# Six gate projections moved among the key and query projections of a hybrid layer, with later query transposes, another order of the first loads and of the last stores

## The chip, the cores and the metric

The kernel runs on one core of a Trainium2 chip. The metric is the time of one execution on the device in microseconds (us). The engines of the core are named as in the profile: PE (TensorE, matrix products; its weight loads are PEld), DVE (VectorE), ACT (ScalarE), POOL (GpSimd) and SP (SyncE, which issues the DMAs here). Each engine works its own instructions off in a fixed order.

## What is computed

One layer of an encoder over 1024 tokens of width 1024, and a final norm. All data are float32.

```python
h = rms_norm(x, mix_norm_w)
proj = h @ w_in
dn_qkv, dn_z, dn_b, dn_a, a_q, a_k, a_v, x_q, gate_logits = jnp.split(proj, IN_OFFSETS, axis=-1)
# A: DeltaNet: conv + SiLU, unit q/k, chunks of 64 with a triangular solve, a scan over
#    16 chunks forward and one backward, norm, SiLU gate                        -> y_dn
# B: attention, 8 query heads, 2 key heads, per-head norm and rotary            -> y_att
# C: cross-attention of 4 heads into 256 memory tokens                          -> y_x
...
ys = jnp.stack([y_dn, y_att, y_x], axis=2)
yb = jnp.einsum("bsnc,ncd->bsnd", ys, w_branch)
gates = jax.nn.sigmoid(gate_logits.reshape(b_, s_, N_BRANCH, D_MODEL))
merged = jnp.sum(gates * yb, axis=2)
x = x + merged @ w_out
x = x + jnp.square(jax.nn.relu(rms_norm(x, ffn_norm_w) @ w_up)) @ w_down
return rms_norm(x, final_norm_w)
```

The triangular solve is per chunk: `triangular_solve(lmat, rhs)` with `lmat` 64 x 64, unit diagonal; there are 128 of them (16 chunks, 4 heads, 2 directions).

## The kernel before

**Products.** Every float32 operand is split into a high and a low part (`split`, L140 to L142: ACT casts the high part, DVE or POOL subtracts it), and a product is three matmuls: high by high, high by low, low by high. `wunit` (L146) loads one unit of weights, 128 columns of all 1024 rows, 512 KB, and splits it; the low part goes to DVE, or to POOL while `wlo[0]` is set. A projection of one unit on one half of the tokens (512) is 24 matmuls of 128x512 into one PSUM tile of the pool `ps_mm`, which has two buffers.

**Order of the program.** The phases are written one after the other, and a scheduler then orders the instructions of each engine by dependencies and modelled times; it may move work of a later phase ahead. Only in attention (from L994 on) is PE's order kept as written.

1. L254 to L285: x is loaded in 8 tiles of 128 tokens, normalised (ACT sums the squares, L223; DVE scales with the norm weight, L278), transposed by PE and split into `hTh[f]`, `hTl[f]` (f: the half of the tokens).
2. L301 to L430: decays, convolution and DeltaNet's matrices per chunk (`conv_tile` L393, `prep` L464), whose results go to device memory (`xs_d`, `kn_d`, `qT_d`, `at_d`).
3. Driver, L663 to L671: one step of `keys()` or `queries()` (24 steps: 8 blocks of keys, 16 of queries), then one step of `other` (the z gate, memory rows and the cross queries, tile `xh`/`xl`). A step projects 128 tokens (`ps_dn`), takes norm and rotary (`rope_norm` L552, on ACT, POOL, DVE), writes the parts `qhl`/`khl`, and the four transposes of them on PE (L84, tile `ps_t`), an eviction on ACT and the stores by SP stand at the head of the next step. `wlo[0]` is POOL here.
4. L693 to L710: the triangular solve, for all 128 chunks at once, one per partition, on DVE: for each of 62 columns a product (L705, tile `tm`) and an addition (L706, tile `X`), then a product with `bcol` (L708). X is loaded from `xs_d` before, stored to `ts_d` after, and read back by chunk as `tf` and `Tr`.
5. L739 to L830: the scan over the chunks (`ps_sp` and `ps_sm` on PE).
6. L870 to L1016: attention, in 64 steps, with cross-attention.
7. L1023 to L1160: the three branch products times gates (y tiles read back as `y_raw`, split into `g_yh`, `g_yl`; gates as `g_l`, through a pool of two buffers), output projection, MLP, final norm, stores.

**Gate projections.** 48 tiles of 24 matmuls (3 branches, 8 units, 2 halves) are written as the generator `gates()`, and `fill(n)` emits its next n matmuls. A finished tile is evicted (tanh, to `g_d`) when the next portion is drawn. 7 tiles are emitted at once after the driver and the scan's code (`GATES[0]`), 3 behind the scan, 33 in portions of 3, 4, 5 and 12 in attention, and the 5 left over in `for _ in gt` (L1019), between attention and the branches.

**Queues.** SP issues all DMAs in one order. A store that isn't ready holds up the loads behind it. At the end the stores of the last two blocks of 128 rows stand in halves in this queue.

Of the kernel before, what the change touches and what calls it, by code (L numbers as in the profile page):

```python
# [9 lines left out]
F32 = mybir.dt.float32  # L10
# [12 lines left out]
GATES = (7, 3)  # L23
# [63 lines left out]
def hybrid_block(tc, x, mem, mix_norm_w, w_in, dn_conv_w, dn_a_log, dn_dt_bias, dn_norm_w, q_norm_w, k_norm_w,  # L87
# [33 lines left out]
    ld(out=ca, in_=ca_d)  # L121
# [5 lines left out]
    act.copy(out=identr, in_=ident)  # L127
# [108 lines left out]
    ld(out=wdn, in_=dn_norm_w.rearrange("o d -> d o"))  # L236
    dve.tensor_scalar(out=wdn, in0=wdn, scalar1=0.5, scalar2=None, op0=ALU.mult)
# [17 lines left out]
    first = {}  # L255
    wbc = p0.tile([P, D], F32, name="wbc", bufs=1)
    for m in range(8):
        if m == 0:
            xts = []
            for i in range(8):  # L260
                xt = p0.tile([P, D], F32, name="xt", tag="xt", bufs=8)
                ld_rows(xt, x, i)
                xts.append(xt)
                if i == 0:
                    ld(out=wbc, in_=mix_norm_w.broadcast_to([P, D]))
                if i == 1:
                    braw = wst.tile([P, 8, 64], F32, name="w_raw", tag="w_raw")
                    bhl = tkp.tile([P, 8, 128], F32R, name="b_hl", tag="t_hi", bufs=1)
                    ld(out=braw, in_=w_in[:, C_BA:C_BA + 64].rearrange("(k p) c -> p k c", p=P))
                    split(bhl[:, :, 0:64], bhl[:, :, 64:128], braw)  # L270
                if i == 3:
                    wlo[0] = gp
                    for ct in (4, 0):
                        first[ct] = wunit(w_in[:, ct * P:(ct + 1) * P], 8, P)
                    wlo[0] = None
# [9 lines left out]
    st.close()  # L285

# [7 lines left out]
    R = [slice(0, 64), slice(64, 128)]  # L294

# [97 lines left out]
    def conv_tile(ct):  # L393
# [4 lines left out]
        for f in range(2):  # L398
            ps = ps_mm()
            proj_ch(ps, wh, wl, f)  # L400
# [175 lines left out]

    def keys():
        wh, wl = wtok(C_AKV)
        for m in range(8):
# [5 lines left out]
            khl = tkp.tile([P, 512], F32R, name="khl", tag="qhl")[:, :384].rearrange("p (g a d) -> p g a d", g=2, a=3)  # L585
            rope_norm(khl[:, :, 1], khl[:, :, 0::2], ps[:, 0:128].rearrange("p (g d) -> p g d", g=2), 2, rope, m, 1.0 / 64, EPS)
            yield
            pst = ps_t(F32R)
# [8 lines left out]
    def queries():  # L597
        for g in range(2):
            wh, wl = wtok(C_AQ + g * 256)
            for m in range(8):  # L600
# [6 lines left out]
                for h in range(4):  # L607
                    pe.transpose(pst[:, h * P:(h + 1) * P], qhl[:, h].rearrange("p a d -> p (a d)"), identr)
# [57 lines left out]
    for _ in other:  # L666
        pass
# [571 lines left out]
```

## Time and profile before

| | us |
|---|---|
| median of 3 runs | 1977.83 (1975.19 to 1977.91) |
| profiled execution | 1976.33 |
| its span | 1974.5 |
| PE busy | 1900.6 (96%) |
| DVE busy | 1169.2 (59%) |
| ACT busy | 731.8 (37%) |
| POOL busy | 397.2 (20%) |

The span is the time from the first to the last record of the profile; the profiled execution's own time is 1.8 us longer. Busy time is the sum over an engine's instructions, and shares are averages over stages that differ much: the table of stretches further below shows that DVE is busy for nearly all of one of them. In a row of the timeline stand the start, the duration, engine, line, operation, output and input, and in brackets the idle time before it with what ended it.

### The profile page before, as it was taken

How to read it: one execution, taken by the hardware profiler on the slowest of the kernel's cores; microseconds unless marked ns; L12 is line 12 of the kernel's file. 1: busy time of each engine (PE TensorE's matmuls, PEld its weight loads, DVE VectorE, ACT ScalarE, POOL GpSimd, SP SyncE). 2: the span in 40 equal slices, each digit the busy share in tenths (PEclk: the TensorE clock that was granted, in tenths of full speed). 3: DMA queues.
4: the chain of work that ended last, by engine and by line, in shares of the span. 5: the costliest groups of instructions: out<-in, count | busy, mean ns of one | idle time of the engine just before them, and what ended most of it. 6: DMA issues, size and time to landing. Idle time of an engine off the chain costs nothing.

```text
span 1974.5 us, 26282 instructions
## 1 busy us (share of the span) xinstructions
PE 1900.6 (96%) x10229; PEld 1611.6 (82%) x10229; DVE 1169.2 (59%) x1701; ACT 731.8 (37%) x1453; POOL 397.2 (20%) x309
## 2 busy tenths in 40 slices
PE   6999897799999999999999999999999999999997
PEld 5888787688998888888888878888888888888885
DVE  4778879993576666666635463444443444444445
ACT  4344343332555666666642131321121212112124
POOL 3003657851251000000000520100010101001013
PEclk9999998899999999999999999999999999999998
DMA  8235743447654222222146455231111102121113
GB/s 170 76 107 149 226 139 110 118 127 243 191 163 133 85 94 75 86 75 86 59 150 201 157 180 161 74 120 40 55 54 33 54 33 65 43 64 46 41 43 86
DMA packets 232893, 207.82 MB, mean 105 GB/s; under 512 B 44800, under 2 KB 196544, under 8 KB 232256
## 3 DMA queue, kind: packets, MB, share of 16 engines
q1 hardware_dynamic: 232768, 206.13, 34.7%
q8 instruction: 81, 1.33, 0.3%
q14 instruction: 44, 0.36, 0.1%
HBM read 148.91 MB, written 57.18 MB: 104 GB/s over the span
## 4 chain that ended last, share of the span: by engine, by line
PE 74%; DVE 6%; POOL 3%; DMA 2%; issue 2%; ACT 1%; SPq 0%; POOLq 0%; DVEq 0%; ACTq 0%
PE ps L81 40%; PE ps_mm L81 20%; PE ps_t L84 3%; PE ps_sm L81 3%; PE ps_t L81 3%; PE ps_s L81 3%; PE ps_sp L81 2%; DVE tm L705 2%; DVE X L706 1%; POOL r_t L560 1%; DMA w_raw<-in_w_out_dram 1%; POOL r_t L561 1%; POOL r_rs L138 0%; DMA X<-xs_d 0%; DVE o L1152 0%
## 5 line engine op out<-in xcount | busy, mean ns | idle before, releaser
L81 PE MATMUL ps_mm<-hTh,w_hi 128*128 128x512 f32 x704 | 286.1, 406 | 3.5 <-ACT hTh L141 3.4
L81 PE MATMUL ps_mm<-hTl,w_hi 128*128 128x512 f32 x704 | 283.9, 404 | 0.0
L81 PE MATMUL ps_mm<-hTh,w_lo 128*128 128x512 f32 x704 | 277.7, 395 | 2.4 <-POOL w_lo L142 2.4
L1140 DVE TENSOR_TENSOR o<-o,ps 128x512 f32<-128x512 f32 (+1 forms) x257 | 171.3, 683 | 97.0 <-PE ps L81 95.5
L81 PE MATMUL ps<-hfh,w_hi 128*128 128x512 f32 x512 | 199.6, 391 | 0.0
L81 PE MATMUL ps<-wdh,al 128*128 128x512 f32 (+1 forms) x514 | 199.6, 389 | 0.0
L81 PE MATMUL ps<-wdl,ah 128*128 128x512 f32 (+1 forms) x514 | 199.6, 389 | 0.0
L81 PE MATMUL ps<-hfl,w_hi 128*128 128x512 f32 x512 | 199.6, 390 | 0.0
L81 PE MATMUL ps<-hfh,w_lo 128*128 128x512 f32 x512 | 199.5, 390 | 0.0
L142 POOL TENSOR_TENSOR wdl<-w_raw,wdh 128x1024 fp32r<-128x1024 f32 x32 | 76.4, 2397 | 601.1 <-ACT wdh L141 601.1
L81 PE MATMUL ps<-wdh,ah 128*128 128x512 f32 (+1 forms) x514 | 188.7, 389 | 0.0
L1132 ACT ACTIVATE f_r<-ps 128x512 f32<-128x512 f32 x64 | 38.1, 595 | 363.7 <-PE ps L81 363.7
L142 DVE TENSOR_TENSOR w_lo<-w_raw,w_hi 128x1024 fp32r<-128x1024 f32 x78 | 100.0, 1282 | 121.0 <-ACT w_hi L141 120.6
L141 ACT CAST w_hi<-w_raw 128x1024 fp32r<-128x1024 f32 x96 | 100.9, 1051 | 171.6 <-PE ps_mm L81 104.0
L1133 DVE TENSOR_TENSOR f_r<-f_r 128x512 f32<-128x512 f32 x64 | 55.3, 865 | 183.3 <-ACT f_r L1132 183.3
L81 PEld LDWEIGHTS ps_mm<-hTh,w_lo 128*128 128x128 f32 x704 | 133.7, 190 | 28.0 <-POOL w_lo L142 2.6
L81 PEld LDWEIGHTS ps_mm<-hTh,w_hi 128*128 128x128 f32 x704 | 133.7, 190 | 27.9 <-ACT hTh L141 3.8
L81 PEld LDWEIGHTS ps_mm<-hTl,w_hi 128*128 128x128 f32 x704 | 133.9, 190 | 20.2
L1072 POOL TENSOR_TENSOR g_acc<-g_acc,g_l 128x512 f32<-128x512 f32 x28 | 41.4, 1481 | 509.8 <-ACT g_yh L141 475.4
L142 DVE TENSOR_TENSOR ptl<-ps_t,pth 128x512 fp32r<-128x512 f32 x128 | 86.6, 687 | 60.0 <-ACT pth L141 59.7
L81 PEld LDWEIGHTS ps<-wdh,al 128*128 128x128 f32 x514 | 96.6, 188 | 19.9
L81 PEld LDWEIGHTS ps<-wdh,ah 128*128 128x128 f32 x514 | 96.5, 188 | 19.8
(288 smaller groups left out, 4045.9 us busy)
## 6 DMA issues: line engine op xcount, KB each, us to landing
w_raw<-in_w_in_dram SPq DMA_DIRECT2D x50, 512.0 KB, 4.1
w_raw<-in_w_up_dram SPq DMA_DIRECT2D x32, 512.0 KB, 4.1
w_raw<-in_w_down_dram SPq DMA_DIRECT2D x32, 512.0 KB, 3.6
g_d<-gt SPq DMA_DIRECT2D x48, 256.0 KB, 2.0
g_l<-g_d SPq DMA_DIRECT2D x24, 512.0 KB, 3.4
w_raw<-in_w_branch_dram SPq DMA_DIRECT2D x12, 512.0 KB, 4.1
y_raw<-y_d SPq DMA_DIRECT2D x12, 512.0 KB, 3.6
xt<-in_x_dram SPq DMA_DIRECT2D x16, 256.0 KB, 9.9
```

The lines of the kernel that those rows point to most:

```text
L81: return self._put(self.tc.nc.tensor.matmul(*a, **k))
L84: return self._put(self.tc.nc.tensor.transpose(*a, **k))
L141: act.copy(out=hi, in_=src)
L142: (eng or dve).tensor_tensor(out=lo, in0=src, in1=hi.bitcast(F32), op=ALU.subtract)
L560: gp.tensor_tensor(out=t1, in0=x0, in1=bc(tab[:, 0, m], 1, nh), op=ALU.mult)
L561: gp.tensor_tensor(out=t2, in0=x0, in1=bc(tab[:, 1, m], 1, nh), op=ALU.mult)
L705: dve.tensor_tensor(out=t, in0=bc(X[:, j + 1:, j], 2, j), in1=bc(X[:, j, 0:j], 1, n), op=ALU.mult)
L706: dve.tensor_tensor(out=X[:, j + 1:, 0:j], in0=X[:, j + 1:, 0:j], in1=t, op=ALU.add)
L1072: (dve if bi == 2 and mt > 5 else gp).tensor_tensor(out=acc[mt][:, c], in0=acc[mt][:, c], in1=t, op=ALU.add)
L1132: act.activation(out=r, in_=ps, func=AF.Relu)
L1133: dve.tensor_tensor(out=r, in0=r, in1=r, op=ALU.mult)
L1140: dve.tensor_tensor(out=o[m][:, c], in0=o[m][:, c], in1=ps, op=ALU.add)
```

## The change

`GATES` is (6, 3). `gates()` and `fill()` are defined ahead of the driver loop, and after every fourth of its 24 steps one gate tile (24 matmuls) is emitted; their weights are split on POOL. With these 6 tiles none is left for L1019. The transposes of a step go into a list `turns` and are emitted two steps later, with four `qhl` and three `qst` buffers. At the start x's first tile is loaded first; the norm weight comes as one row and is spread by two matmuls with a row of ones and two copies; the units for channels 4 and 0 are loaded between x's tiles; the b and a columns and `wdn` come after x; and the first half of the projections for 4 and 0 is emitted ahead of the decays. At the end blocks 6 and 7 get their factors first, then 7 and 6 are scaled, and the first half of each is stored through ACT's queue.

```diff
-GATES = (7, 3)
+GATES = (6, 3)
...
+    xts = [p0.tile([P, D], F32, name="xt", tag="xt", bufs=8) for _ in range(8)]
...
+    ld_rows(xts[0], x, 0)
+    ld(out=wrow, in_=mix_norm_w)
+    ld(out=ca, in_=ca_d)
+    for i in range(1, 4):
+        ld_rows(xts[i], x, i)
+    for c in range(0, D, 512):
+        ps = ps_mm()
+        pe.matmul(ps, lhsT=one1, rhs=wrow[:, c:c + 512], start=True, stop=True)
+        act.copy(out=wbc[:, c:c + 512], in_=ps)
+    act.copy(out=identr, in_=ident)
+    wlo[0] = gp
+    first[4] = wunit(w_in[:, 4 * P:5 * P], 8, P)
+    for i in range(4, 6):
+        ld_rows(xts[i], x, i)
+    first[0] = wunit(w_in[:, 0:P], 8, P)
+    for i in range(6, 8):
+        ld_rows(xts[i], x, i)
...
-                if i == 0:
-                    ld(out=wbc, in_=mix_norm_w.broadcast_to([P, D]))
...
+    head = {}
+    for ct in (4, 0):
+        head[ct] = ps_mm()
+        proj_ch(head[ct], *first[ct], 0)
...
+    turns = []
+
+    def turn(hl, nh, put):
+        def go():
+            pst = ps_t(F32R)
+            for i, part in enumerate(nh(hl)):
+                pe.transpose(pst[:, i * P:(i + 1) * P], part.rearrange("p a d -> p (a d)"), identr)
+            st = xp.tile([P, 512], F32R, name="qst", tag="qst", bufs=3)
+            act.copy(out=st, in_=pst.bitcast(F32))
+            put(st)
+        turns.append(go)
...
-    for _ in chain(keys(), queries()):
-        next(other, None)
...
+    for i, _ in enumerate(chain(keys(), queries())):
+        next(other, None)
+        if i % 4 == 3:
+            fill(24)
+        if i > 1:
+            turns.pop(0)()
...
+    def store(q, m, c):
+        for h, j in enumerate((m, 15 - m)):
+            q.dma_start(out=out[j * 64:(j + 1) * 64, c], in_=o[m][h * 64:(h + 1) * 64, c])
+
...
+        if m > 5:
+            store(act, m, slice(0, 512))
...
+        if m > 5:
+            store(nc.sync, m, slice(512, 1024))
+        else:
             ld_rows(o[m], out, m, store=True)
...
+    for m in (6, 7):
+        rs3[m] = factor(m, len(cs) - 7 + m)
+    finish(7)
     finish(6)
-    finish(7)
```

SP's queue at the place where the solve's input is loaded: `xs_d` is its source in device memory, `kab` and `qst` are keys on their way out, `vt` values. Before:

```order
L97 DMA at_d7_117<-dd_1968 128x512
L97 DMA vz_d_124<-vt_2235 128x128
L97 DMA vz_d_124<-vt_2326 128x128
L97 DMA xs_d_118<-dd_1968 64x8x64 x2
L97 DMA ka_d_122<-kab_2121 256x1x128
L97 DMA kb_d_123<-kab_2121 256x1x128
L97 DMA vz_d_124<-vt_2411 128x128
L97 DMA X_4243<-xs_d_118 128x4096
```

And in the changed kernel:

```order
L97 DMA at_d7_115<-dd_1977 128x512
L97 DMA vz_d_122<-vt_2226 128x128
L97 DMA vz_d_122<-vt_2317 128x128
L97 DMA xs_d_116<-dd_1977 64x8x64 x2
L97 DMA X_4436<-xs_d_116 128x4096
L97 DMA bcol_4438<-bt_d_118 8x1x64 x2
L97 DMA ka_d_120<-qst_2288 256x1x128
L97 DMA kb_d_121<-qst_2288 256x1x128
```

The key stores stand behind the load of X now.

PE's queue around the first scan matmul (`ps_sp` from `tf`; the next takes `Tr`, which ACT copies from its result). Before, where `ps_mm_5893`, `5927` and `5955` are gate projections of 24 matmuls each:

```order
L81 MATMUL ps_mm_5927<-hTl0_151,w_hi_5921 128x512
L81 MATMUL ps_sp_4433<-ca_73,tf_4422 64x64 x4
L81 MATMUL ps_mm_5927<-hTh0_149,w_lo_5922 128x512
...
L81 MATMUL ps_mm_5955<-hTl1_152,w_hi_5921 128x512
L81 MATMUL ps_sp_4442<-vn_4426,Tr0_4406 128x128 x4
L81 MATMUL ps_sp_4459<-ca_73,tf_4448 64x64 x4
L81 MATMUL ps_mm_5955<-hTh1_150,w_lo_5922 128x512
```

And in the changed kernel, where `ps_t_4423` are the transposes of the last block of queries, and `ps_mm_4195` and `4280` projections of 24 matmuls:

```order
L84 MATMUL ps_t_4423<-identr_74,qhl_4259 128x128 x4
L81 MATMUL ps_mm_4195<-hTh0_147,w_hi_4190 128x512
...
L81 MATMUL ps_mm_4280<-hTh1_148,w_lo_4191 128x512
L81 MATMUL ps_sp_4626<-ca_73,tf_4615 64x64 x4
L81 MATMUL ps_sp_4635<-vn_4619,Tr0_4599 128x128 x4
L81 MATMUL ps_sp_4652<-ca_73,tf_4641 64x64 x2
L81 MATMUL ps_mm_4314<-hTh1_148,w_hi_3928 128x512
```

The matmuls on `Tr` follow those on `tf` at once. Counted over PE's queue from the end of DeltaNet's preparation to the first matmul of the scan, 397 matmuls of 128x512 stand there before and 356 in the changed kernel. DVE's queue from the first column step of the solve to its last product has 225 instructions before and 215 in the changed kernel; inside the scan PE's queue goes 12 times from scan matmuls to gate matmuls or back before, and 75 times in the changed kernel.

PE's queue behind the last attention matmul (`vz`: values). Before, the five remaining gate projections end with `ps_mm_10262`, and the first branch product follows:

```order
L81 MATMUL ps_mm_10262<-hTl1_152,w_hi_10228 128x512
L81 MATMUL ps_mm_10262<-hTh1_150,w_lo_10229 128x512
L81 MATMUL ps_mm_10331<-g_yh_10300,w_hi_10326 128x512
L81 MATMUL ps_mm_10331<-g_yl_10301,w_hi_10326 128x512
L81 MATMUL ps_mm_10331<-g_yh_10300,w_lo_10327 128x512
L81 MATMUL ps_mm_10331<-g_yh_10306,w_hi_10326 128x512
```

And in the changed kernel, where `g_yh_10309`, `10315`, `10321` are the first three y tiles:

```order
L81 MATMUL ps_t_10266<-pth_10215,vz_4593 128x256
L81 MATMUL ps_t_10266<-ptl_10216,vz_4593 128x256
L81 MATMUL ps_mm_10340<-g_yh_10309,w_hi_10335 128x512
L81 MATMUL ps_mm_10354<-g_yh_10309,w_hi_10335 128x512
L81 MATMUL ps_mm_10340<-g_yl_10310,w_hi_10335 128x512
L81 MATMUL ps_mm_10340<-g_yh_10309,w_lo_10336 128x512
L81 MATMUL ps_mm_10340<-g_yh_10315,w_hi_10335 128x512
```

The first branch products follow attention at once, and two of them run side by side.

## Rows read from the trace of the kernel before

**Rows 1.** The page's part 1: busy time, share of the span, instructions of each engine.
```profile
PE 1900.6 (96%) x10229; PEld 1611.6 (82%) x10229; DVE 1169.2 (59%) x1701; ACT 731.8 (37%) x1453; POOL 397.2 (20%) x309
```

**Rows 2.** Stretches: length, busy time (instructions) of each engine, clock, DMA share, GB/s.
```profile
0.00:38.00 38.00, 18.91 (x86) 15.59 (x87) 19.84 (x33) 20.15 (x36) 11.48 (x19) 1.00 0.92 215
272.00:432.00 160.00, 130.18 (x866) 120.00 (x865) 155.01 (x173) 62.02 (x221) 118.41 (x85) 0.91 0.40 117
432.00:480.00 48.00, 47.96 (x221) 39.23 (x220) 29.02 (x42) 11.45 (x24) 9.44 (x12) 1.00 0.73 233
560.00:640.00 80.00, 77.75 (x528) 68.56 (x527) 56.85 (x119) 41.65 (x98) 24.77 (x22) 0.98 0.51 149
1010.00:1117.00 107.00, 107.00 (x481) 89.01 (x480) 48.46 (x52) 25.87 (x29) 18.52 (x13) 1.00 0.57 183
1945.00:1974.50 29.50, 15.43 (x74) 12.84 (x72) 21.75 (x35) 14.27 (x36) 12.52 (x14) 0.81 0.58 143
```

**Rows 3.** Waits of PE from 258 to 432: total us, times, longest.
```profile
PE ps_t L84 <- DVE qhl L573: 20.5, 7, 7.6
```

**Rows 4.** Groups by line from 258 to 432: busy us, mean ns, idle before.
```profile
L705 DVE TENSOR_TENSOR tm<-X 128x720 f32<-128x720 f32 (+30 forms) x48 | 60.0, 1249 | 5.6 <-DMA X<-xs_d 5.1
L142 POOL TENSOR_TENSOR w_lo<-w_raw,w_hi 128x1024 fp32r<-128x1024 f32 x12 | 33.3, 2774 | 8.9 <-ACT w_hi L141 8.6
```

**Rows 5.** Timeline of DVE inside the solve and at its end.
```profile
291.01 0.87 DVE L705 TENSOR_TENSOR tm<-X 128x686 f32<-128x686 f32 x1
291.91 2.94 DVE L706 TENSOR_TENSOR X<-X,tm 128x686 f32<-128x686 f32 x1
...
439.75 1.22 DVE L142 TENSOR_TENSOR w_lo<-w_raw,w_hi 128x1024 fp32r<-128x1024 f32 x1
...
441.55 0.68 DVE L142 TENSOR_TENSOR xl<-ps_mm,xh 128x512 fp32r<-128x512 f32 x1
...
454.44 4.43 DVE L708 TENSOR_TENSOR X<-X,bcol 128x4096 f32<-128x4096 f32 x1
```

**Rows 6.** Timeline of SP's DMA queue around the solve.
```profile
253.52 1.26 SPq L97 DMA_DIRECT2D xs_d<-dd  x2
...
257.97 0.34 SPq L97 DMA_DIRECT2D X<-xs_d  x1
...
458.89 0.32 SPq L97 DMA_DIRECT2D ts_d<-X  x1
...
465.62 0.65 SPq L97 DMA_DIRECT2D tf<-ts_d  x1
```

**Rows 7.** DMA issues from 455 to 480: KB each, median us to landing.
```profile
tf<-ts_d SPq DMA_DIRECT2D x3, 64.0 KB, 4.0
```

**Rows 8.** The chain of waits from 436 to 480: start, us, what.
```profile
442.28 31.36 PE ps_mm L81 x137
473.64 0.60 PE ps_sp L81 x8
```

**Rows 9.** Timeline of POOL beside the column steps of rows 5.
```profile
291.53 5.52 POOL L142 TENSOR_TENSOR w_lo<-w_raw,w_hi 128x1024 fp32r<-128x1024 f32 x2 [0.16 <-ACT w_hi L141]
```

**Rows 10.** Groups of DVE by line and shape from 267 to 459.
```profile
L142 DVE TENSOR_TENSOR xl<-ps_mm,xh 128x512 fp32r<-128x512 f32 x8 | 5.5, 682 | 0.0
```

**Rows 11.** Timeline of ACT behind the first scan matmul.
```profile
474.34 0.36 ACT L760 COPY Tr<-ps_sp 64x256 f32<-64x256 f32 x1 [3.19 <-PE ps_sp L81]
```

**Rows 12.** Timeline of ACT behind the last attention matmul.
```profile
1014.60 2.00 ACT L141 CAST g_yh<-y_raw 128x1024 fp32r<-128x1024 f32 x2
```

**Rows 13.** The page's part 6, DMA issues: KB each, median us to landing.
```profile
g_l<-g_d SPq DMA_DIRECT2D x24, 512.0 KB, 3.4
...
y_raw<-y_d SPq DMA_DIRECT2D x12, 512.0 KB, 3.6
```

**Rows 14.** Timeline of PE in the scan, a visit of three gate matmuls.
```profile
496.03 0.48 PE L81 MATMUL ps_mm<-hTh,w_hi 128*128 128x512 f32 x1
...
496.90 1.16 PE L81 MATMUL ps_sm<-u,ke 64*128 64x128 f32 x8
```

**Rows 15.** Timeline of SP's queue at the end.
```profile
1950.00 21.82 SPq L97 DMA_DIRECT2D out_dram<-o  x18
```

More of the change, by code (lines that the diff above doesn't have):

```diff
@@ L120, in hybrid_block @@
     ca = con.tile([P, CA_N], F32, name="ca")
-    ld(out=ca, in_=ca_d)
     ident = ca[:, CA_ID:CA_ID + 128]
@@ L255, in hybrid_block @@
     first = {}
+    xts = [p0.tile([P, D], F32, name="xt", tag="xt", bufs=8) for _ in range(8)]
     wbc = p0.tile([P, D], F32, name="wbc", bufs=1)
-    for m in range(8):
[L258 to L263, printed above, removed]
-                if i == 0:
-                    ld(out=wbc, in_=mix_norm_w.broadcast_to([P, D]))
[L266 to L275, printed above, removed]
+    wrow = p0.tile([1, D], F32, name="wrow", bufs=1)
+    one1 = p0.tile([1, P], F32, name="one1", bufs=1)
+    gp.memset(one1, 1.0)
+    ld_rows(xts[0], x, 0)
[15 more added lines that the diff above has]
+        ld_rows(xts[i], x, i)
+    wlo[0] = None
+    for m in range(8):
         xt = xts[m]
@@ L285, in hybrid_block @@
     st.close()
+    braw = wst.tile([P, 8, 64], F32, name="w_raw", tag="w_raw")
+    bhl = tkp.tile([P, 8, 128], F32R, name="b_hl", tag="t_hi", bufs=1)
+    ld(out=braw, in_=w_in[:, C_BA:C_BA + 64].rearrange("(k p) c -> p k c", p=P))
+    split(bhl[:, :, 0:64], bhl[:, :, 64:128], braw)
+    ld(out=wdn, in_=dn_norm_w.rearrange("o d -> d o"))
+    dve.tensor_scalar(out=wdn, in0=wdn, scalar1=0.5, scalar2=None, op0=ALU.mult)
     def proj_tok(ps, wh, wl, m):
@@ L398, in conv_tile @@
         for f in range(2):
-            ps = ps_mm()
-            proj_ch(ps, wh, wl, f)
+            ps = head.pop(ct, None) if f == 0 else None
+            if ps is None:
+                ps = ps_mm()
+                proj_ch(ps, wh, wl, f)
             pv = ps.rearrange("p (m h c) -> p m h c", h=2, c=64)
@@ L661, in memory @@
             yield
-    other = chain(gate_z(), mem_norm(), memory(), queries_x())
-    for _ in chain(keys(), queries()):
-        next(other, None)
-    for _ in other:
-        pass
-    mst.close()
-    tst.close()
-    wlo[0] = None
     def gates():
@@ L689, in fill @@
             next(gt, None)
+    other = chain(gate_z(), mem_norm(), memory(), queries_x())
+    for i, _ in enumerate(chain(keys(), queries())):
[4 more added lines that the diff above has]
+            turns.pop(0)()
+    for _ in other:
+        pass
+    for go in turns:
+        go()
+    mst.close()
+    tst.close()
+    wlo[0] = None
     sst = ExitStack()
@@ L1203, in hybrid_block @@
                         gp.tensor_tensor(out=o[m][:, c], in0=o[m][:, c], in1=lwb[:, c], op=ALU.mult)
-            if last:
+            if last and m < 6:
                 rs3[m] = factor(m, len(cs))
-                if m < 6:
-                    finish(m)
+                finish(m)
+    for m in (6, 7):
+        rs3[m] = factor(m, len(cs) - 7 + m)
+    finish(7)
     finish(6)
-    finish(7)
     top.close()
```

38 lines of the change are left out of this document (12 added, 26 removed).

## Prediction

> **What bounds the kernel now.** I read the busy line and the slices first [rows 1]: TensorE (PE) is busy for 1900.6 of 1974.5 us, so 74 us is all that better filling could ever give, and every matmul that is moved to a place where PE is already busy costs its full time. The table of stretches [rows 2] shows where the 74 us lie: 19.1 in the first 38 us, 29.8 from 272 to 432, 2.3 in 560 to 640, 14.1 after 1945. From 1010 to 1117 there is none. So the question is what sets the end of the stretch 272 to 432.
>
> There PE waits for DVE: 20.5 us in seven waits of the query transposes for the query halves [rows 3]. In the same stretch DVE is busy for 155.01 of 160 us [rows 2]. What fills it is the triangular solve, two instructions of equal size for each of 62 columns: 48 of the first kind take 60.0 us [rows 4], the second kind as much; then one product of 4.43 us at 454.44 [rows 5]. Until it has ended, at 458.87, nothing of the scan can start: X is stored at 458.89, loaded back as tf at 465.62 [rows 6], 4.0 us to landing [rows 7], about 469.7. So **DVE's chain of column steps sets when the scan's data exist**. PE itself is at work from 432 to 480 without a gap [rows 2], and its first scan matmul stands at 473.64 behind 137 projection matmuls without a break in its own queue [rows 8]: the queue is 3.9 us later than the data. These two, DVE's chain and what PE's queue holds ahead of the first scan matmul, are nearly level; whichever is later in the changed kernel decides.
>
> POOL makes the solve longer. A pair of weight splits on POOL takes 5.52 us from 291.53 [rows 9]; the column step that runs beside the first takes 2.94 us where its twin of the same size took 0.87 [rows 5]. A split on POOL thus costs DVE about 2.07 us, though DVE does nothing of it; the same split on DVE costs 1.22 [rows 5].
>
> **Start.** Before the last tile of x, the change leaves out the broadcast of the norm weight (512 KB) and moves the 256 KB of b and a columns behind x. At the 215 GB/s of that stretch [rows 2] that is 0.75 MB, 3.5 us. Two head projections (24 matmuls each) stand ahead of the convolution; before, one of them was fitted in. PE idles 19.1 us there, so the additional 24 fit: 24 x 0.229 = 5.5 us, with the 0.229 from 137 matmuls in 31.36 us [rows 8]. But ACT takes the sums of squares and the casts of hT in one queue, and what it has to cast does not shrink. Ends 0 and -5.5; nothing in the rows lies nearer to one of them, so I take the middle, **-2.7**, which is below the 3.5 of the bytes.
>
> **Load of X.** Before, the load stands behind two key stores and a value store, issued at 257.97, 3.2 us after the last store of its source had been issued at 253.52 plus 1.26 [rows 6]. In the changed order it follows that store at once. It still has to wait until that store has landed, which these rows don't show apart. Ends 0 and -3.2; **-0.5**, since a wait on a store just issued is likely to take most of those 3 us.
>
> **Solve.** Between the first column step and the last product DVE's queue holds 225 instructions before and 215 after. Gone: two weight splits (1.22 each, -2.4), five of eight splits of the cross-query projections (5 x 0.68, -3.4) [rows 5, 10] and one query's four rope steps (256 columns or fewer, so between 0 and 4 x 0.68: half, -1.4); one tanh-gate product of 512 columns comes in (0.7, taken as a split of that size). POOL has 13 weight splits in it instead of 12, +2.1. Sum **-4.4**. Ends 0 (more splits of gate weights meet longer column steps) and -9 (twice).
>
> A rule of the Trainium skill bears on that price. The row above has 2.07 us lost per POOL split of about 2.77 us [rows 4]. The page titled "SBUF — State Buffer", section "Who interferes with whom", says that VectorE with two SBUF inputs and GpSimd share one read interface as an exclusive lock, the loser blocked for the whole instruction. By it, handing the gate weights' splits to POOL saves DVE nothing, and the thirteenth split would cost 2.8 instead of 2.1; the sum would be -3.7. The trace shows the loss, a little below a full block, and I keep the row's 2.1.
>
> **From the end of the solve to the scan.** In the new order the last query's transposes follow the solve (their DVE half is queued behind the product), then come two whole projections of 24, which share one free PSUM buffer because a gate tile holds the other until the next portion is emitted, then the first scan matmul. 2 x 5.5 us plus the transposes and two evictions that PE has to sit out is about 16 us from the end of X, against 14.8 (458.87 to 473.64): +1.3. Directly behind it stands the matmul that needs the copied Tr; before, 21 projection matmuls lay between. The copy starts at 474.34 and takes 0.36 [rows 11]; PE was free at 473.64 + 0.60 [rows 8], so +0.7 with the way back. **+2.0**; ends -1 (no eviction waited for) and +2.6.
>
> **Work that is moved behind the scan's start.** Six gate projections run inside the solve, but the two that stood there anyway and two cross-query projections do so no longer: between the end of the DeltaNet preparation and the first scan matmul PE's queue holds 397 matmuls of 128x512 before, 356 after. Since the scan's start hangs on DVE, what PE does in those 30 idle us is free, but the 41 that are now behind it run where PE has no idle time: 41 x 0.229 = **+9.4**. This is the step a reader should look at twice: filling the idle time would pay only if the later stretches lost as much work, and here the number of matmuls ahead of the scan falls.
>
> **Attention to branches.** Before, five gate projections (5 x 24 x 0.229 = 27 us) run after attention, while ACT casts the first two y tiles, from 1014.60 [rows 12], and the other two later; PE is busy for all 107 us of that stretch [rows 2]. Afterwards no gate projection is left there. After the last attention matmul ACT has a last attention block to copy, then a tile of another branch, y0 and y1 (2.00 for two such casts): the first branch matmul can start 2.5 us late, with its low halves 1.2 later. y2 and y3 use the buffers of y0 and y1, so their loads are issued when g_yl is made (about +4), 3.6 us to landing [rows 13], cast and split (1.0 and 1.2) one after the other: +10 to +11. The gate rows that the first evictions need wait for the same two buffers: issued at +10.5, 3.4 us to landing [rows 13], +13.9, eviction 0.7. Only then has PE a buffer for the third projection. It has 5.5 us of work in that time: **+9.1**. Ends 5 (y2 and y3 early) and 12.
>
> **Switches in the scan.** PE changes between scan and gate matmuls 12 times before and 75 times after. A visit of three gate matmuls at 496.03 holds PE 0.87 us to the next scan matmul at 496.90 instead of 3 x 0.229 = 0.69 [rows 14], so 0.1 per switch: 63 x 0.1 = 6.3 at most, 0 if the switches they save elsewhere weigh as much. **+3.1**, the middle.
>
> **The rest.** The 2.3 us of idle time in the scan's last part [rows 2] may be filled: **-1.5**. At the end SP's queue issues 18 output stores in 21.8 us, 1.2 each, until 1971.8 [rows 15]. Of the last eight the change gives four to ACT's queue; the last scaling bounds what that saves to about two of these times, and I take a little less: **-2.0** (-1 to -2.5). The transposes two steps behind take 20.5 us of waits off PE, but in the stretch that DVE bounds: 0.
>
> Sum: -2.7 - 0.5 - 4.4 + 2.0 + 9.4 + 9.1 + 3.1 - 1.5 - 2.0 = **+12.5**. The profiled execution took 1976.33, so 1988.8; the median of the runs is 1.5 above it, so 1990.3. I say 1990.
>
> **Rivals.** *Faster.* The solve isn't the bound I take it for: PE's queue is the later of the two (473.64 against data at 469.7, and the chain of waits there is PE alone [rows 8]). Then the scan starts earlier by whatever PE gains: the start in full (-5.5), the solve -9, the load -0.5, no price at the scan's start; 9.4 for moved work stays, switches and the branches' start are hidden by loads that were issued early. -5.5 - 0.5 - 9 + 9.4 - 1.5 - 2 = -9.1: 1967 for the profiled execution, 1969 for the median. For it: the level race, and a mean granted clock of 0.91 of full speed from 272 to 432 [rows 2], between the levels of 1.2 and 2.4 GHz, that steady gate work would lift. Against it: a higher clock inside a stretch that DVE bounds gives nothing.
> *No change.* The scan starts 9 us earlier instead of 4.4, the branch stall is at its low end of 5 and switches are free: 12.5 - 4.6 - 4.1 - 3.1 = +0.7, 1978.5 for the median.
> *The change doesn't do what it says*, in that the scheduler leaves the gates where they were: excluded, the queue shows them among the queries.
>
> **How the numbers follow.** Forecast (slower, scan start bound by DVE, PE uncovered at the branches) 0.69; faster 0.18; no change 0.13. Each case spreads over the bounds; all bounds on the good side together give about 1968, on the bad side some 2005. The range that leaves 2 in 10 outside reaches into the faster case: 1971 to 1999; of the forecast alone 1981 to 2000. About 0.2% (4 us) is what a measurement of this kernel can tell from no change: faster 0.18, same 0.13, slower 0.69.
>
> **What would show it.** Right: the solve ends 5 to 10 us earlier than 458.87 and the first scan matmul comes 14 to 16 us behind it; PE idles at least 5 us just after the last attention matmul; PE's idle time from 272 to the scan stays above 20 us although the waits for query halves shrink. Wrong: the first scan matmul more than 15 us before 473.64, PE busy without a gap between attention and branches, or a scan that isn't longer in spite of its additional matmuls.

## The result and the profile after

The changed kernel takes 2004.98 us (median of 4 runs, 2000.51 to 2007.71) against 1976.51 before (1971.65 to 1977.91): a ratio of 1.0146, 95% interval 1.0119 to 1.0173. It is slower by 28 us; the forecast was 12. The profiled execution has a span of 2005.9 us against 1974.5, so 31.4 us are to be found in its trace. Of the four executions of e15, below, one ran at a granted clock of 0.75 and took 2370.8 us; its ratio leaves that one out.

The page's busy line of the changed kernel, to set beside [rows 1]:

```profile
PE 1921.5 (96%) x10233; PEld 1618.1 (81%) x10233; DVE 1178.9 (59%) x1698; ACT 732.9 (37%) x1455; POOL 406.1 (20%) x313
```

PE has four matmuls more and is busy for 20.9 us longer; its idle time is 84.4 us instead of 73.9. The product work is the same but for those four, so the busy time grew because matmuls took longer. The table of stretches tells where. First the changed kernel, in the columns of [rows 2] (length, busy time of PE, PEld, DVE, ACT, POOL, granted clock, DMA share, GB/s):

```profile
0.00:38.00 38.00, 22.05 (x83) 16.98 (x84) 24.47 (x31) 19.98 (x36) 17.37 (x21) 0.91 0.89 206
258.00:480.00 222.00, 187.17 (x1127) 165.55 (x1126) 191.49 (x233) 78.55 (x266) 138.93 (x109) 0.92 0.45 135
1000.00:1130.00 130.00, 123.17 (x597) 101.34 (x596) 70.98 (x94) 50.62 (x77) 8.62 (x6) 0.95 0.45 146
```

The two later stretches in the kernel before:

```profile
258.00:480.00 222.00, 191.67 (x1177) 171.42 (x1175) 190.75 (x236) 79.03 (x265) 131.67 (x105) 0.94 0.49 149
1000.00:1130.00 130.00, 130.00 (x590) 108.15 (x589) 56.15 (x62) 30.01 (x36) 25.07 (x18) 1.00 0.55 179
```

In the stretch of the solve PE's idle time did not shrink although six gate projections (144 matmuls, 33 us) were put into it: 34.8 us instead of 30.3, at a lower clock. Behind attention, where there was no gap, stand 6.8 us of idle time and a clock of 0.95.

The milestones (us from the span's start) let the difference be followed:

| | before | after | later by |
|---|---|---|---|
| load of X issued | 258.0 | 258.1 | +0.2 |
| X stored (solve ended) | 458.9 | 455.5 | -3.4 |
| first scan matmul | 473.6 | 476.5 | +2.9 |
| last scan matmul (`ps_sm`) | 601.5 | 645.7 | +44.2 |
| last attention matmul | 1013.8 | 1053.8 | +40.0 |
| first branch matmul | 1035.7 | 1056.6 | +20.9 |
| output projection begins | 1167.3 | 1199.1 | +31.8 |
| last matmul begins | 1960.1 | 1992.9 | +32.8 |
| end | 1974.5 | 2005.9 | +31.4 |

The scan alone holds 216 projection matmuls instead of 55, which is 37 of its 41 us; attention holds 24 less, and the 96 behind attention are gone. Net, 41 more run behind the first scan matmul, as the order showed. At the 0.229 us of the row that the forecast used they come to 9.4 us; this is a count with a price, no run tested it apart.

A second account, by what PE lost, serves for the experiments too, which are told further below (e1 to e15). "Clock" is PE's busy time times (1 - granted clock), summed over the table of stretches in steps of 2 us; "rest" is the span without idle time and clock, against the kernel before.

| | span | idle | of it 258 to 480 | of it 1000 to 1130 | clock | rest |
|---|---|---|---|---|---|---|
| before | 1974.5 | 73.9 | 30.3 | 0.0 | 13.9 | 0 |
| after | 2005.9 | 84.4 | 34.8 | 6.8 | 24.2 | +10.6 |
| gates alone (e1) | 2004.5 | 85.8 | 36.9 | 7.3 | 22.9 | +9.1 |
| after, cover (e5) | 1984.5 | 76.9 | 37.0 | 0.0 | 18.8 | +2.1 |
| before, splits on DVE (e7) | 1961.3 | 61.5 | 15.5 | 0.0 | 11.7 | +1.4 |
| after, splits on DVE (e9) | 1980.0 | 64.8 | 16.4 | 6.2 | 18.3 | +10.2 |
| after, cover and splits on DVE (e11) | 1959.6 | 59.7 | 17.6 | 0.3 | 8.6 | +4.6 |
| after, gate tiles evicted early (e12) | 1992.5 | 79.1 | 32.3 | 7.0 | 24.2 | +2.5 |
| all but gates, splits on DVE (e13) | 1955.0 | 55.0 | 14.0 | 0.0 | 12.0 | +1.3 |
| after, early eviction and cover (e14) | 1980.4 | 75.5 | 31.0 | 0.0 | 15.1 | +3.1 |
| after, early eviction, cover, splits on DVE (e15) | 1951.8 | 52.0 | 12.0 | 0.0 | 12.5 | +0.6 |

So the 31.4 us are 10.5 of idle time, 10.3 of lower clock and 10.6 of rest.

### The profile page after: what moved, and what is told of

Same layout as the page of the kernel before. It is cut to its first block, busy times and chain, and to the rows that moved or that the text cites. A ratio compares the mean times of both kernels' runs of the same rounds, so it can differ in the third digit from the quotient of the medians.

```text
span 2005.9 us, 26271 instructions
## 1 busy us (share of the span) xinstructions
PE 1921.5 (96%) x10233; PEld 1618.1 (81%) x10233; DVE 1178.9 (59%) x1698; ACT 732.9 (37%) x1455; POOL 406.1 (20%) x313
## 4 chain that ended last, share of the span: by engine, by line
PE 62%; issue 9%; DVE 9%; DMA 3%; POOL 3%; ACT 1%; SPq 0%; POOLq 0%; ACTq 0%; DVEq 0%
PE ps L81 30%; PE ps_mm L81 18%; PE ps_sm L81 3%; PE ps_t L84 3%; PE ps_t L81 3%; PE ps_s L81 3%; DVE tm L733 2%; DVE X L734 2%; PE ps_sp L81 2%; POOL wdl L140 1%; DMA w_raw<-in_w_down_dram 1%; DMA w_raw<-in_w_up_dram 1%; DVE r_x L583 1%; DMA w_raw<-in_w_out_dram 1%; DVE r_x L581 0%
## 5 line engine op out<-in xcount | busy, mean ns | idle before, releaser
L81 PE MATMUL ps_mm<-hTh,w_hi 128*128 128x512 f32 x704 | 291.0, 414 | 10.6 <-DVE z_th L647 4.8
L81 PEld LDWEIGHTS ps<-wdl,ah 128*128 128x128 f32 x514 | 96.5, 188 | 19.9
```

The lines of the kernel that those rows point to most:

```text
L81: return self._put(self.tc.nc.tensor.matmul(*a, **k))
```

## Where the time went, in the trace of the changed kernel

**From the solve to the scan.** The chain of waits from 440 to 482, cut (start, us, what):

```profile
452.34 3.15 POOL rsq_t L135
455.57 1.15 POOL r_rs L136
456.74 2.57 DVE r_x L583
459.38 0.41 ACT qhl L584
459.82 0.44 DVE qhl L586
...
460.39 0.72 PE ps_t L84 x4
461.12 8.35 PE ps_mm L81 x24
469.49 0.59 ACT xh L139
470.11 0.70 DVE xl L140
...
475.01 2.37 DMA tf<-ts_d
...
477.88 0.37 ACT Tr L788
478.29 1.53 PE ps_sp L81 x12
```

X's last product ends at 455.44, but the last query's factors are still on their way through POOL; its split into `qhl` ends at 460.2, and PE, whose queue has that query's transposes next, stands from 455.2 to 460.4. Two of these steps are far longer than others of their shape in this stretch. `rsq_t` on POOL takes 3.15 us (median of 16: 0.57) and ends with X's product, which DVE had begun before it. `r_x` on DVE takes 2.56 us (median 0.42) beside a weight split that POOL began just before it:

```profile
456.68 2.33 POOL L140 TENSOR_TENSOR w_lo<-w_raw,w_hi 128x1024 fp32r<-128x1024 f32 x1
456.74 2.56 DVE L583 TENSOR_TENSOR r_x<-r_x,r_rs 128x256 f32<-128x256 f32 x1 [0.91 <-POOL r_rs L136]
```

Then 24 matmuls take 8.35 us instead of 5.5. The stretches of 5 us from 455 show why:

```profile
455.00:460.00 5.00, 0.16 (x1) 0.00 (x0) 3.57 (x5) 1.63 (x3) 4.92 (x6) 0.99 0.79 338
460.00:465.00 5.00, 4.61 (x13) 3.74 (x14) 0.94 (x2) 0.86 (x2) 0.88 (x2) 0.50 0.89 292
465.00:470.00 5.00, 4.45 (x16) 3.21 (x14) 0.00 (x0) 0.51 (x1) 0.00 (x0) 0.83 0.77 226
470.00:475.00 5.00, 4.15 (x18) 3.45 (x19) 0.69 (x1) 0.07 (x1) 0.17 (x1) 1.00 0.66 221
```

After 5 us of idleness the granted clock is 0.50, the 1.2 GHz level, and comes back to 2.4 GHz in the stretch from 465 to 470. From the product's end to the first scan matmul (476.5) it is 21.1 us, against 14.8 before.

**Behind attention.** The chain of waits from 1050 to 1085, from the last attention matmuls on:

```profile
1052.18 1.92 PE ps_t L81 x16
...
1054.57 1.05 ACT g_yh L139
...
1056.79 1.23 DVE g_yl L140
...
1058.04 4.89 DMA y_raw<-y_d
...
1062.99 1.05 ACT g_yh L139
...
1064.07 1.24 DVE g_yl L140
...
1065.32 4.84 DMA g_l<-g_d
...
1070.26 0.70 DVE g_acc L1097
...
1071.00 14.05 PE ps_mm L81 x54
```

These are the steps of the forecast one by one: y0 split, y2 loaded into its buffer, cast, split, then g_l into that buffer, the eviction, and only then the third projection. PE is free at 1054.1 and goes on without a gap from 1071.0. Two sizes were off: the loads landed after 4.9 and 4.8 us, not 3.6 and 3.4 [rows 13], and from 1054 to 1080 PE's mean clock was 0.74.

```profile
1054.00:1080.00 26.00, 19.21 (x58) 13.82 (x58) 13.73 (x15) 9.59 (x10) 0.00 (x0) 0.74 0.66 217
```

From the last attention matmul to the output projection it takes 145.3 us, against 153.4 before of which 21.6 were gate projections: 13.4 us more. By the second account 6.8 us of idle time and 5.6 of lower clock lie between 1000 and 1130.

**The start.** The timelines of POOL, DVE and PE at three places:

```profile
15.91 2.34 POOL L140 TENSOR_TENSOR w_lo<-w_raw,w_hi 128x1024 fp32r<-128x1024 f32 x1
15.97 3.36 DVE L279 SCALAR_TENSOR_TENSOR xt<-xt,rs,wbc 128x1024 f32<-128x1024 f32 x1 [0.44 <-POOL rs L136]
...
23.42 2.36 POOL L140 TENSOR_TENSOR w_lo<-w_raw,w_hi 128x1024 fp32r<-128x1024 f32 x1
23.48 3.38 DVE L279 SCALAR_TENSOR_TENSOR xt<-xt,rs,wbc 128x1024 f32<-128x1024 f32 x1 [0.45 <-POOL rs L136]
```
```profile
29.99 0.78 PE L81 MATMUL ps_mm<-hTl,w_hi 128*128 128x512 f32 x1
30.56 0.63 PE L81 MATMUL ps_mm<-hTh,w_lo 128*128 128x512 f32 x1
```

x does come earlier, but two of DVE's normalisations take 3.4 us instead of 1.3, while POOL splits the two weight units; PE waits for them, and goes on with the head projections at 30.0 us (30.2 before), at half clock for the first of them (0.43 us from start to start instead of 0.23).

## The experiments

In kernels whose program is the same up to there, X's load is issued at 258.0 (before) and 255.6 us (e4), and at 258.1 (changed), 256.1 (e5) and 256.4 us (e6); a shift of 2 us of one milestone says nothing. The times below are compared with runs of the kernel before on the same chip.

**Which part.** Each part of the change alone, on the kernel before.

e1, the gates:

```diff
-GATES = (7, 3)
+GATES = (6, 3)
...
+    for i, _ in enumerate(chain(keys(), queries())):
+        next(other, None)
+        if i % 4 == 3:
+            fill(24)
```

> The kernel before with the gate part alone: six gate projections among keys and queries, GATES (6, 3); transposes, start and end as before. Theory (the gate part makes the loss: 65 fewer projection matmuls ahead of the scan, 65 x 0.229 = 14.9 us, branches uncovered 13 us, switches 4 us, the solve some 4 us shorter): about 28 us slower than before, PE idle or at its lower clock just after the last attention matmul. Rival (the loss comes from the end of the solve and the start as changed by the other parts): 10 to 15 us slower.

2004.56 us, 1.0145 (1.0125 to 1.0164): the whole loss, as the theory had it. The scan starts earlier here (470.6, 12.6 us behind the solve's end at 458.0), so the long way from the solve to the scan isn't the gates' own; in its place 65 matmuls less stand ahead of the scan.

e2, the start:

```diff
+    ld_rows(xts[0], x, 0)
+    ld(out=wrow, in_=mix_norm_w)
...
+    head = {}
+    for ct in (4, 0):
+        head[ct] = ps_mm()
+        proj_ch(head[ct], *first[ct], 0)
```

> The kernel before with the new start alone (order of x's loads, norm weight as a row, head projections). Theory (PE's head start is given back by transposes that stand behind the head projections and by DVE's normalisations beside POOL's splits): within 2 us of before, X's load issued at 257 to 259 us. Rival (the prediction's step): 2.7 us faster, X's load issued near 255.

1975.39 us, 0.9998 (0.9988 to 1.0008); load of X at 256.6. The prediction's -2.7 would be 0.9986, just outside the interval.

e3, the transposes two steps behind:

```diff
+    for i, _ in enumerate(chain(keys(), queries())):
+        next(other, None)
+        if i > 1:
+            turns.pop(0)()
```

> The kernel before with the transposes two steps behind alone. Theory (DVE's solve bounds that stretch, so PE's shorter waits bring nothing): within 2 us of before, waits of the transposes for query halves down from 20.5 us to under 12. Rival (the last queries then come behind the solve's end and hold up the scan): 4 to 8 us slower, first scan matmul 4 us or more behind 473.6.

1973.69 us, 0.9990 (0.9981 to 0.9999). The waits for query halves fall from 20.5 to 4.7 us and those for memory, value and cross-query tiles take their place. Within the 2 us that the theory allowed.

e4, the end:

```diff
+        if m > 5:
+            store(act, m, slice(0, 512))
...
+        if m > 5:
+            store(nc.sync, m, slice(512, 1024))
```

> The kernel before with the new end alone (blocks 6 and 7, stores on two queues). Theory: 1.4 us faster, as the time from the last matmul's start to the end was 13.0 us in the changed kernel and 14.4 before. Rival (the scheduler's other order moves more than the end): no gain or more than 3 us either way.

1973.11 us, 0.9987 (0.9978 to 0.9996): 1 to 4 us faster.

e8, the edits of e3 and e4 together on the kernel before.

> The kernel before with the transposes two steps behind and the new end, nothing else of the change. Theory (the two parts, 0.1% and 0.13% alone, add up): 4 to 5 us faster than before. Rival (both alone were lucky orders of the scheduler, or noise): within 2 us of before.

1974.45 us, 0.9995 (0.9980 to 1.0011): the gains of single parts are at the edge of what can be measured; they didn't add up.

**What of the gate part costs.** On the changed kernel.

e5, five gate projections kept for the place behind attention:

```diff
-GATES = (6, 3)
+GATES = (1, 3)
```

> The changed kernel with GATES (1, 3) in place of (6, 3): five gate projections less are emitted at once, so that 96 matmuls are left between attention and the branches, as before, and the scan holds 96 projection matmuls instead of 216. Theory (of the 28 us, 13 are branches without cover and 4 are switches in the scan; the work ahead of the scan stays at 1032 matmuls): 1986 to 1990 us, PE without a gap from the last attention matmul to the first branch product. Rival (the missing cover isn't the cost, the loads come late whatever stands ahead): still 2000 us or more.

1986.36 us, 1.0056 (1.0036 to 1.0077), in the theory's range. From the last attention matmul to the output projection it takes 153.3 us, as before (153.4), and PE has no idle time from 1000 to 1130 and full clock:

```profile
1000.00:1130.00 130.00, 129.96 (x604) 107.96 (x603) 59.61 (x67) 35.46 (x45) 18.30 (x14) 1.00 0.54 176
```

Against e1 or the changed kernel the account shows 7 to 9 us of idle time gone, 4 to 5 of clock and 7 to 8.5 of rest. The switches between scan and projection matmuls fell from 82 and 75 to 18. Inside the scan alone, PE's time without idle time, lower clock and 0.229 us for each projection matmul is 117.0 us in e1, 116.3 in the changed kernel and 110.7 here: 0.1 us per switch. The remaining 1 to 3 us of the rest lie outside the scan.

e6, one instruction moved:

```diff
-    gp.memset(X.rearrange("p r c -> p (r c)")[:, 0::65], 1.0)
+    dve.memset(X.rearrange("p r c -> p (r c)")[:, 0::65], 1.0)
```

> The changed kernel with one instruction, the writing of X's diagonal after the last column step, on DVE in place of POOL. In the trace of the changed kernel it stands in POOL's queue ahead of the last query's rope products, which so wait for the solve's end, and with them that query's transposes and PE. Theory (this wait makes the way from the solve's end to the first scan matmul 21.1 us instead of 14.8): way down to 15 to 17 us, time 4 to 6 us less than the changed kernel, near 2000. Rival (the loads of tf and Tr in SP's queue, behind stores of the cross queries, bound it anyway): less than 2 us gained.

2002.42 us, 1.0140 (1.0120 to 1.0161). From X's store to the first scan matmul it is still 19.7 us (453.6 to 473.3). My theory fell: the last query's rope products do come earlier on POOL, but then `rsq_t` takes 3.66 us there and again ends with X's product (453.5), and the query's next steps on DVE stand behind that product anyway. The rival's time fits, its reason doesn't: PE waits 4.9 us for the query, until 458.5, works off the transposes and 48 projection matmuls with one gap of 1.4 us, and goes on to the first scan matmul without a wait for tf.

e12, a gate tile evicted with its last matmul:

```diff
-                    for _ in gemm_steps(ps, [(gh[:, k], gl[:, k], hTh[f][:, k], hTl[f][:, k]) for k in range(8)]):
-                        yield
+                    steps = gemm_steps(ps, [(gh[:, k], gl[:, k], hTh[f][:, k], hTl[f][:, k]) for k in range(8)])
+                    for i, _ in enumerate(steps):
+                        if i < 23:
+                            yield
                     act.activation(out=t, in_=ps, func=AF.Tanh, scale=0.5)
                     ld(out=g_d[b][mt][:, f * 512:(f + 1) * 512], in_=t)
+                    yield
```

> The changed kernel, but a finished gate tile is evicted and stored with its last matmul instead of at the next portion, so that it doesn't hold one of the two PSUM buffers for four steps. 1152 instead of 1032 projection matmuls then stand ahead of the scan and 96 instead of 216 in it. Theory (the held buffer makes every other projection wait for its predecessor's eviction, which is where the gates' own gain in the solve's stretch goes): idle time and lower clock from 258 to 480 fall from 35 and 14 us by 15 to 25 together, time 1980 to 1990 us. Rival (DVE's solve and not the buffer limits the stretch): the 120 matmuls only delay the scan's start by their 27 us, time 2000 us or more.

1991.35 us, 1.0081 (1.0065 to 1.0097). The theory's time is just missed and its reason fails: idle time and clock from 258 to 480 fall by 5 us together, not by 15 to 25. The rival's time fails too, though its reason is nearer to what the trace shows. X is stored at 455.0, as early as in the changed kernel, but the first scan matmul stands at 496.1, behind the additional projections:

```profile
474.31 10.53 PE ps_mm L81 x46
...
485.13 10.99 PE ps_mm L81 x48
496.13 0.60 PE ps_sp L81 x8
```

What is gained, 13.6 us, is mostly rest (8 us). The scan has 36 switches instead of 75, which at 0.1 us each are half of that; the other half isn't explained.

**What keeps PE idle beside the solve.**

e7, on the kernel before, the low parts of the weights that are loaded in the stretch of keys and queries made on DVE:

```diff
-    wlo[0] = gp
+    wlo[0] = None
```

> The kernel before with the weights' low parts in the stretch of keys and queries made on DVE instead of POOL. Theory (a split on POOL costs the solve 2.07 us, on DVE 1.22; the solve sets the stretch): 12 weight splits and 4 of the memory's save 10 to 14 us of the solve, which then ends 180 to 190 us after its load's issue instead of 201; the time falls by about as much as PE's idle time there, 6 to 12 us. Rival (PE's queue, not the solve, sets the scan's start): the solve is shorter and the time within 3 us of before.

1960.97 us, 0.9929 (0.9908 to 0.9950): 14 us faster than the kernel before. But the solve was only 4.5 us shorter (196.4 us from the issue of X's load to its store, instead of 200.9), not 10 to 14. The column steps did get shorter, groups by line from 258 to 475 in the kernel before and in this one:

```profile
L706 DVE TENSOR_TENSOR X<-X,tm 128x62 f32<-128x62 f32 (+30 forms) x62 | 68.3, 1102 | 1.1
L705 DVE TENSOR_TENSOR tm<-X 128x62 f32<-128x62 f32 (+30 forms) x62 | 68.0, 1096 | 5.9 <-DMA X<-xs_d 5.1
```
```profile
L706 DVE TENSOR_TENSOR X<-X,tm 128x62 f32<-128x62 f32 (+30 forms) x62 | 56.3, 908 | 1.0
L705 DVE TENSOR_TENSOR tm<-X 128x62 f32<-128x62 f32 (+30 forms) x62 | 55.6, 897 | 1.7 <-DMA ka_d<-kab 0.8
L142 DVE TENSOR_TENSOR w_lo<-w_raw,w_hi 128x1024 fp32r<-128x1024 f32 x17 | 21.8, 1280 | 2.0 <-ACT w_hi L141 1.9
```

24 us less for 16 POOL splits gone (12 of `w_lo`, 4 of `t_lo`), 1.5 us each, and about as much again, 22 us, for the splits that DVE now does itself (17 of `w_lo` instead of 4, and 4 of `t_lo`). The 14 us came from elsewhere: PE's idle time in the stretch, 30.3 us before, is 15.5. Waits of PE from 258 to 475:

```profile
PE ps_sp L81 <- DMA tf<-ts_d: 6.8, 2, 6.6
PE ps_t L84 <- DVE khl L575: 6.4, 2, 4.5
...
PE ps_t L84 <- DVE qhl L573: 1.8, 5, 0.5
```

The 20.5 us of waits for query halves [rows 3] are down to 1.8. The longest single wait is now the one for tf: PE has done what there is to do, 1128 instead of 1073 projection matmuls ahead of the scan, and waits for the solve's result. In the kernel before, POOL's timeline shows what a query step meets:

```profile
338.17 1.79 POOL L138 TENSOR_TENSOR r_rs<-rsq_t,mhalf 128x4 f32<-128x4 f32 x1
339.93 2.39 POOL L142 TENSOR_TENSOR w_lo<-w_raw,w_hi 128x1024 fp32r<-128x1024 f32 x1
342.41 0.25 POOL L137 TENSOR_SCALAR rsq_t<-r_ss 128x4 f32<-128x4 f32 x1
```

The rotary products and factors of a query are small steps on POOL, ACT and DVE, one after the other; a weight split of 2.3 to 3.3 us stands in POOL's queue between them, and PE waits at the transposes. Over the 16 queries the way from the copy out of PSUM to the finished `qhl` is 14.2 us on average (longest 24.1) before and 10.9 (15.2) in e7. Of the 3.3 us between them 2.7 are waits just ahead of POOL's steps; the steps of POOL and DVE themselves got shorter by 0.4 to 0.5 each.

e9, the same edit on the changed kernel.

> The changed kernel with the weights' low parts in the stretch of keys and queries on DVE. Theory (POOL's splits beside the solve, not the gate projections, keep PE's 35 us of idle time there; without them 1104 instead of 1032 projection matmuls stand ahead of the scan): 15 to 20 us faster than the changed kernel, 1985 to 1990 us, idle time from 258 to 480 near 18 us; the uncovered branches stay, with their 12 us of idle time and lower clock. Rival (splits of six more weight units on DVE make the solve so long that nothing is won): 2000 us or more.

1981.40 us, 1.0023 (1.0013 to 1.0034): 24 us faster than the changed kernel, more than expected. Idle time from 258 to 480 is 16.4 us, and the way from X's store to the first scan matmul is 13.5 us instead of 21.1; what stays is the uncovered place behind attention (6.2 of idle time, 5.5 of clock) and the switches. What PE waited for there in the changed kernel was not the queries above all (waits of PE from 258 to 480):

```profile
PE ps_t L84 <- DVE qhl L586: 10.0, 3, 5.2
PE ps_mm L81 <- POOL w_lo L140: 6.4, 2, 5.7
PE ps_mm L81 <- DVE z_th L647: 4.8, 3, 2.4
```

The longest of the 10.0 us is the last query behind the solve; next come weights of the memory's projections whose low part POOL was late with, and PSUM tiles of the z gate that DVE hadn't read out yet. In e9 0.9 us of waits for queries and 1.4 for low parts are left.

e11, the edits of e9 and e5 on the changed kernel.

> The changed kernel with both: those splits on DVE and GATES (1, 3), so that 96 gate matmuls are left as cover between attention and branches. Theory (the two losses are independent: 18 us for the cover, 15 to 20 for the splits): 1966 to 1972 us, faster than the kernel before, but no better than the same splits without the gate part (1961). Rival (gates among the queries gain once the solve is shorter): under 1958.

1961.68 us, 0.9934 (0.9919 to 0.9949): as with the splits alone (e7). That comparison came out as the theory had it; its time was 4 us too long, since it reckoned with 15 to 20 us for the splits and e9 has 24. The measured 18.6 (e5) and 23.6 us (e9) do add up.

e13, everything but the gate part, with the splits on DVE; on the changed kernel, beside the edit of e9:

```diff
-GATES = (6, 3)
+GATES = (7, 3)
...
-        if i % 4 == 3:
-            fill(24)
```

> All of the change but the gate part (GATES (7, 3), none among the queries), with those splits on DVE. Theory (start 0, transposes and end 1 to 2 us each, splits 14): 1957 to 1961 us, the fastest so far by a little. Rival (transposes two steps behind and the splits take away the same waits): 1961 us, as with the splits alone.

1956.01 us, 0.9901 (0.9887 to 0.9916): 1 us below the theory's range, and 5 us below e7; the two intervals still overlap.

e14, the edits of e12 and e5 on the changed kernel.

> The changed kernel with the early eviction and GATES (1, 3): 1128 projection matmuls ahead of the scan, none in it, 96 behind attention. Theory (lost: 10 to 12 us of idle time and lower clock at the uncovered branches; 8 us of switches in the scan; the rest idle time and lower clock in the solve's stretch that the gates among the queries add): 1977 to 1982 us, so with both mended the gates still gain nothing against before. Rival (buffer and cover are all that is wrong with gates among the queries): 1970 us or less, faster than before.

1982.26 us, 1.0032 (1.0021 to 1.0043): just above the theory's range. With the buffer and the cover mended the gates still cost 4 to 8 us. PE's idle time beside the solve is 31.0 us, as before; the account spreads the cost over idle time, clock and rest (1.6, 1.2 and 3.1 us), and what causes it stays open.

e15, the edits of e5, e9 and e12 on the changed kernel.

> The changed kernel with all three: early eviction, GATES (1, 3), weights' low parts in that stretch on DVE. Theory (once the splits are on DVE, PE's idle time there is 14 us with or without gates among the queries): 1957 to 1962 us, no better than the same without the gate part (1956). Rival (with buffer, cover and splits mended the gates fill what idle time is left): under 1952 us.

1954.21 us, 0.9890 (0.9853 to 0.9926): 3 us below the theory's range and above the rival's, faster than both kernels, and not to be told apart from e13. Gates among the queries neither gain nor lose then. The 12.0 us of idle time that are left there hold one wait of 7.1 us for tf.

## Why the prediction was wrong

The direction held, and so did the mechanism of the two largest terms; the size, 12.5 us, was less than half of the 28 measured. The step that failed most is one that the sum doesn't have: every gap of PE was priced at full clock afterwards, and lower clock made 10.3 of the 31.4 us. Step by step, in the profiled executions:

| step | forecast | measured |
|---|---|---|
| start and load of X | -3.2 | +0.2 |
| solve, load to store | -4.4 | -3.6 |
| solve's end to the scan | +2.0 | +6.3 |
| 41 matmuls behind the scan's start | +9.4 | +9.4 (counted, same price) |
| branches without cover | +9.1 | +13.4 |
| switches, idle time filled in scan | +1.6 | +4.3, and +1.3 in attention |
| end | -2.0 | -1.3 |
| MLP | 0 | +0.9 |
| sum | +12.5 | +30.9 (the span: +31.4) |

The first row is a step that failed outright. "Nothing in the rows lies nearer to one of them, so I take the middle" put a gain where the rows had the reason against it: the loss of a DVE step beside a POOL split [rows 5, 9], which I used for the solve, applies to the normalisations of x as well, and the change moves POOL's splits beside them. e2 has the start at 0. The middle between two ends isn't a measurement. The load of X, put at -0.5, can't be told from the 2 us by which its place shifts from run to run.

The third row is a term mis-sized. I let the last query's parts be ready right behind X's product, but steps of POOL, DVE and ACT were still open: 4.8 us, not some tenths, 2.1 of them in one DVE step that ran beside a weight split on POOL. And both there and behind attention I priced the gaps as time in which PE does nothing, at full clock afterwards. A gap of 5.2 us was followed by 24 matmuls in 8.35 us. The prediction has no term for the 10.3 us of lower clock. Rows that I had read showed it, a clock of 0.91 from 272 to 432 beside 29.8 us of gaps [rows 2]. That row stood in the prediction as an argument for the rival.

The fifth row was right in its mechanism, link by link, and e5 took it away; the two landings were 1.3 and 1.4 us longer than the medians in [rows 13], and 5.6 us of lower clock came on top of 6.8 of idle time.

Switches cost what the row of three matmuls [rows 14] said or a little less: inside the scan PE's time without idle time, lower clock and the projections' 0.229 us is 111.4 us before and 116.3 in the changed kernel, 0.08 us per switch, and e5 has 0.1. That is 4.8 us against 3.1 forecast; halving the 6.3, for switches saved elsewhere, had no row behind it. The idle time of the scan, which was to be filled for -1.5, grew from 2.3 to 3.4 us.

The solve's term was nearly right. The premise under it, that DVE's chain sets when the scan's data exist, holds in e7 and e15, where PE waits 7 us for tf. In the changed kernel PE's queue was the later of the two: it stood for the last query and then went from projections to the first scan matmul without a wait. But "DVE bounds that stretch, so what PE does in the idle time is free" missed what the idle time was made of: in the kernel before PE stood still mostly because single query steps came late through POOL (20.5 of 30.3 us). The seven waits of [rows 3] were in the prediction, and were set to 0 as hidden behind the solve. For the later transposes alone the 0 stands: in e3 most of these waits are gone, others take their place, and the time moves by 0.1%. But the idle time as a whole was not hidden. In e7, without POOL's splits, 55 more projection matmuls pass ahead of the scan and the kernel gains 14 us with a solve that is only 4.5 us shorter. Read so, the six gates among the queries could not fill that time: PE takes its queue in order, and a gate tile ahead of a transpose doesn't bring the query. In the changed kernel the waits for queries are fewer (10.0 us), and waits for the low parts of the memory's weights on POOL (6.4 us, 2.4 before) and others stand in their place. That POOL's splits are the reason in the changed kernel too was tried in e9 (24 us). How they delay the rest, by the order of POOL's queue or by slower steps, is shown for the query steps alone, where POOL's queue is 2.7 of 3.3 us; for the other waits it stays open.

Of the prediction's own signs two came and two did not. PE did idle at least 5 us behind attention (6.8), and its idle time from 272 to the scan stayed above 20 us (31.9). The solve ended 3.4 us earlier, not 5 to 10, and the first scan matmul came 21.1 us behind it, not 14 to 16.

The rule that I cited of the Trainium skill, page "SBUF — State Buffer", section "Who interferes with whom", has the loser blocked for the whole instruction. Single rows come near to that: the two normalisations at the start lost 2.1 us each beside splits of 2.34 and 2.36 us, the column step of [rows 5] 2.07. Averaged over the 16 splits that e7 took off POOL the column steps lost 1.5 us per split, of 2.8 to 3.1. So 2.1 was too high as a price for every split; what lowers the average is not shown.

## What to carry to other kernels

Before work is moved into an engine's idle time, ask what each gap waits for: an in-order queue whose next instruction waits for a slow chain stays as idle with more work behind it, and the chain (here, before the change, small steps queued behind large splits on POOL) is what has to be shortened. Work that stands at a change of phase may be the cover of the next phase's loads; taking the last of it away cost 13 us here, 5.6 of them through the clock. Where a change opens a gap on PE, give the clock that follows it a term of its own: here a gap of 5.2 us cost 2.9 us more in the 24 matmuls behind it.

## What the runs showed that was not expected

- After 5.2 us without a matmul PE was granted 1.2 GHz, and 24 matmuls of 128x512 took 8.35 us instead of 5.5.
- Moving 16 weight splits from POOL, where one takes 2.8 to 3.1 us, to DVE, where it takes 1.3, leaves DVE's own total almost the same (24 us of shorter column steps against 22 us of added splits) and makes the kernel 14 us faster; on the changed kernel 24 us.
- Two DMAs of 512 KB behind attention landed after 4.8 and 4.9 us, where the medians of the kernel before are 3.4 and 3.6; the longest of its kind there took 4.5.
- A step of 128x4 elements on POOL took 3.15 us beside DVE's product of 128x4096, and 3.66 in e6, and ended with it both times.
